# A hybrid encoder trunk on one core: the dots of the matrix memory's modulation issued with the third and fourth head's values only, each kept in its place, and two gate steps two products later

## The chip, the cores and the metric

The kernel is one program on one core of a Trainium2 chip. Its time is the device time of one execution in microseconds (us), as the median of the runs shown. A profile is one execution taken by the hardware profiler; its times are counted from the first instruction of the program. The engines are named as in the profile: PE is TensorE, PEld its weight load, DVE VectorE, ACT ScalarE, POOL GpSimd, SP SyncE, which issues the loads and stores.

## The reference

The trunk has two layers over 1024 tokens of width 1024, all in float32. The first mixes tokens by latent attention, the second by a matrix memory; each is followed by a gated MLP. Every sub-layer takes a modulation from the conditioning vector: a shift, a scale and a gate, which are six products of one vector with a 1024 x 1024 matrix per layer. Of the second layer, this is what the change touches (cut):

```python
mod = c_act @ mod_w[i] + mod_b[i]
sh_a, sc_a, g_a, sh_f, sc_f, g_f = [t[:, None, :] for t in jnp.split(mod, 6, axis=-1)]
h = rms_norm(x) * (1 + sc_a) + sh_a
...
proj = h @ w_in
q, k, v, o, gates = jnp.split(proj, [qk_w, 2 * qk_w, 2 * qk_w + v_w, 2 * qk_w + 2 * v_w], axis=-1)
i_pre, f_pre = gates[..., :H], gates[..., H:]
log_f = jax.nn.log_sigmoid(f_pre)
bc = lax.cumsum(gate_chunks(log_f), axis=3)
...
C_new = decay[..., None, None] * C + jnp.einsum('bhs,bhsv,bhsd->bhvd', ws, vt, kt)
```

The matrix memory has four heads, with 128 wide keys and 256 wide values. For each head the sequence is gone through in chunks; from chunk to chunk a state C is carried, weighted by what the gates give. While the second layer's memory is computed, the kernel also has to compute three of its modulation vectors: the gate `g_a` of this sub-layer, and the scale and shift of the MLP behind it.

## The kernel before, in words

**Products.** Everything is computed from float32 split into a high and a low part (`whi` and `wlo` for weights). Each product of 128 rows is three matmuls (`mm3`, lines 175 to 177): high by high, high by low, low by high. A weight of 128 x 1024 comes by `unit`: a 512 KB load into a raw buffer `wraw`, a copy on ScalarE to the high part (line 167), a subtraction on VectorE to the low part (line 168). In this part of the program there are two raw buffers and four pairs of split ones.

**Order.** The code is written in the order in which it should run, but a list scheduler with its own picture of durations sets the final order of each engine, and it may move an instruction ahead of others. `tc.keep_in_program_order` keeps an instruction where the code has it. Each engine, SyncE too, runs its instructions strictly in the final order.

**Modulation dots.** `mod_dot` (line 198) is one VectorE instruction over 128 x 1024 numbers: a piece of the modulation matrix, loaded into a tile `mraw`, times the activated conditioning vector (`crow`, here a copy `crow2`), summed to one number per partition. `mod_steps` yields after each; eight of them give one vector, and `mod_bias` ends it (line 203). In the matrix memory `mraw` takes a buffer of the same ring of two as `wraw`. The 24 dots of this part are drawn two at a time (`piece(mods, 2)`) behind each of the four groups of the values of the second, third and fourth head. They aren't kept in order.

**The matrix memory.** The first head's values and the gates' raw numbers are computed first, then the four gate steps run on small tiles, each put off until a number of products (`GATES`) has been issued: `gates0` makes sums and maxima along the rows (ending in the scan of line 1562), `gates1` transposes their ends (`gr`, line 1566) and makes the maxima carried from chunk to chunk, `gates2` makes weights from them and stores two of them to memory (`gd`, line 1587), `gates3` transposes the weights to columns (`gcol`). `need(gcol)` runs whatever step is still put off when the first 20 products of the next query and key (`inp`) are through. The two stored rows come back as broadcasts (`load_rows`, line 1414: into `crow` and into `ib`, which has one buffer).

Per head there are then:
- the values (`v_proj`): four groups of 16 products of 256 columns into `vp`, each split into the tile `va` (lines 608 and 609)
- the preparation (`prep`) of two halves of the sequence, placed behind the second and the third group: the scores `st`, the transposed keys `kp`, the weighted and split `pT`, `qw` and `kw`
- the chain (`chain`): eight steps, each with products into `po` and, but for the last, `pc`, a new state C on VectorE (lines 1466 and 1468), its high part on ScalarE (1471) and its low part on VectorE (1472)
- between the chain's steps, pieces of other products, here called the cover: the output gate (`ogate`, tile `inp`, two weights for a head), which needs nothing of the chain
- query and key of the next head, and `finish`, which transposes the result (`yT`).

Of the kernel before, what the change touches and what calls it, by code (L numbers as in the profile page):

```python
# [42 lines left out]
WARM = 14  # L43
W0, W0_RSTD, WF, WF_RSTD = (6, 10), (4, 3), (4, 5), (4, 6)
SHARE = 7
GATES = (2, 16, 20, 24)
MODS = (0,) * 4 + (2,) * 11 + (3,)
BS = 3
K_SSQ, K_ROWS, K_ROPE, K_NORM = 2, 4, 3, 3
# [48 lines left out]
def trunk_kernel(ctx: ExitStack, tc: tile.TileContext, xT, pos, c_d, cols_d, mod_w, win, winT, w0, w1, wf, wd, out):  # L98
# [98 lines left out]
    def mod_dot(l, i, raw, c=None):  # L197
        return dve.scalar_tensor_tensor(raw, raw, 1.0, crow if c is None else c, ALU.mult, ALU.mult, accum_out=modc[l][:, i:i + 1])
# [6 lines left out]
    def mod_steps(parts, raw_tile, c=None):  # L205

        for l, j in parts:
            for k in range(KT):
                raw = raw_tile()
                nc.sync.dma_start(raw, mod_w[l, j * 8 + k])  # L210
                if c is None:
                    yield
                    tc.keep_in_program_order(mod_dot(l, j * 8 + k, raw))
                else:
                    mod_dot(l, j * 8 + k, raw, c)
                    yield
            mod_bias(l, j * 8, KT)

# [552 lines left out]
    mods = mod_steps(((0, 2), (0, 4), (0, 3)), lambda: mod_raw())  # L771
# [32 lines left out]
    def piece(gen, n=1):  # L804
        for _ in range(n):
            next(gen, None)
# [478 lines left out]
    mods = mod_steps(((0, 5), (1, 1), (1, 0)), lambda: pF[0].tile([P, D], F32, tag="mraw", bufs=1, name=nm("mraw")))  # L1285
# [79 lines left out]
    def v_proj(hd):  # L1365
        va = va_tiles()
        uv = [unit(w1[U_MV + 2 * hd + i]) for i in range(2)]
        yield va
        for t2 in range(4):
            ps = mm_tile("vp")  # L1370
            for j in range(2):
                t = 2 * t2 + j
                tsl = slice((t % 4) * P, (t % 4 + 1) * P)
                for k in range(KT):
                    rs = [x[:, (k % 4) * 256:(k % 4 + 1) * 256] for x in uv[k // 4]]
                    mm3(ps[:, j * 256:(j + 1) * 256],
                        (h[t // 4][0][:, k, tsl], h[t // 4][1][:, k, tsl]), rs, k == 0, k == KT - 1)
            ps3 = ps.rearrange("p (a b) -> p a b", a=2)
            split_ps(va[0][:, 2 * t2:2 * t2 + 2, 0:256], va[1][:, 2 * t2:2 * t2 + 2, :], ps3)
            piece(mods, 2)  # L1380
            yield va

    def in_steps(u, hf, evac):
# [394 lines left out]
```

## Time and profile before

| | |
|---|---|
| three runs, median | 2217.82 us (2212.6 to 2218.76) |
| the profiled execution | 2215.57 us |
| its span, first to last instruction | 2213.9 us |
| mean granted TensorE clock | 0.992 |
| TensorE matmuls busy | 2169.1 us, 98% |
| VectorE busy | 1698.4 us, 77% |
| the 56 dots that load into `mraw` | median 1.219 us each |

The rows of the profile name the line, the engine, the operation, the tile written and the tiles read. Behind a bar stand a group's busy time, the mean of one in ns, and the engine's idle time just before, with what ended it. In a timeline a row begins with its start and its length, and a bracket gives the idle time before it and what ended that. In a table by windows a row begins with the window, its length, and for each engine the busy time with the number of instructions, then the granted clock, the share of the DMA engines that was busy, and GB/s.

### The profile page before, as it was taken

What the parts mean: (1) busy time and instruction counts of PE and PEld (TensorE: products, weight loads), DVE (VectorE), ACT (ScalarE), POOL (GpSimd) and SP (SyncE); (2) the same over time, 40 slices, a digit from 0 to 9 for tenths busy, and PEclk for the clock granted to TensorE, in tenths of its full rate; (3) what the DMA queues carried; (4) which work ended last, traced back from release to release, by engine and by line L of the source; (5) the groups of instructions that cost most, each with busy time, mean ns of one, the idle gap of its engine ahead of it and who ended that gap; (6) DMA issues with size and microseconds to landing.
All of it is one profiled execution on the core that took longest, in us unless ns stands there. A gap on an engine that the chain in (4) does not pass through costs nothing.

```text
span 2213.9 us, 28734 instructions
## 1 busy us (share of the span) xinstructions
PE 2169.1 (98%) x10553; PEld 1819.7 (82%) x10553; DVE 1698.4 (77%) x2754; ACT 1045.3 (47%) x1812; POOL 200.4 (9%) x232
## 2 busy tenths in 40 slices
PE   9999999999999999999999999999999999999997
PEld 7878888887888888778888888988788888877886
DVE  8877788669878776999974755466887777689996
ACT  6466566456444444443353434344554444444335
POOL 0000000000000000242210111010000000022222
PEclk9999999999999999999999999999999999999998
DMA  8412334832444442543133342354243332245122
GB/s 315 151 50 64 99 101 154 281 114 66 158 140 141 132 131 80 190 150 99 48 114 104 104 130 70 119 176 149 67 134 100 110 124 96 82 157 205 43 66 77
DMA packets 105085, 270.50 MB, mean 122 GB/s; under 512 B 12336, under 2 KB 15984, under 8 KB 104944
## 3 DMA queue, kind: packets, MB, share of 16 engines
q1 hardware_dynamic: 104544, 268.28, 37.1%
q8 instruction: 83, 1.36, 0.3%
q14 instruction: 58, 0.48, 0.1%
q10 hardware_dynamic: 400, 0.39, 0.1%
HBM read 221.53 MB, written 44.47 MB: 120 GB/s over the span
## 4 chain that ended last, share of the span: by engine, by line
PE 87%; DVE 7%; DMA 2%; ACT 1%; issue 1%; POOL 0%; SPq 0%; DVEq 0%; POOLq 0%; ACTq 0%
PE pa L177 7%; PE pa L175 7%; PE pa L176 7%; PE pd L175 4%; PE pd L176 4%; PE pd L177 4%; PE sc L677 3%; PE da L175 3%; PE da L177 3%; PE da L176 3%; PE op L175 3%; PE op L177 3%; PE op L176 3%; PE db L177 2%; PE inp L177 2%; PE inp L175 2%
## 5 line engine op out<-in xcount | busy, mean ns | idle before, releaser
L992 ACT ACTIVATE whi<-raw 128x512 fp32r<-128x512 f32 (+1 forms) x252 | 147.5, 607 | 262.4 <-PE pb L176 61.0
L992 ACT ACTIVATE whi<-wsum 128x512 fp32r<-128x512 f32 (+1 forms) x224 | 133.9, 617 | 184.1 <-PE pa L176 61.5
L175 PE MATMUL pa<-T,whi 128*128 128x512 f32 x528 | 206.6, 391 | 5.0 <-DVE g L1080 5.0
L177 PE MATMUL pa<-T,wlo 128*128 128x512 f32 x528 | 206.5, 391 | 3.1 <-DVE wlo L993 3.1
L176 PE MATMUL pa<-T,whi 128*128 128x512 f32 x528 | 205.9, 390 | 0.0
L993 DVE TENSOR_TENSOR wlo<-wsum,whi 128x512 fp32r<-128x512 f32 (+1 forms) x224 | 150.7, 686 | 33.2 <-ACT whi L992 31.8
L993 POOL TENSOR_TENSOR wlo<-raw,whi 128x512 fp32r<-128x512 f32 (+1 forms) x96 | 140.8, 1480 | 382.6 <-ACT whi L992 341.2
L175 PE MATMUL da<-U,whi 128*128 128x512 f32 (+1 forms) x364 | 139.8, 384 | 2.2 <-ACT whi L992 2.2
L176 PE MATMUL da<-U,whi 128*128 128x512 f32 (+1 forms) x364 | 139.1, 382 | 0.0
L177 PE MATMUL da<-U,wlo 128*128 128x512 f32 (+1 forms) x364 | 138.4, 382 | 0.0
L993 DVE TENSOR_TENSOR wlo<-raw,whi 128x512 fp32r<-128x512 f32 (+1 forms) x156 | 104.7, 678 | 24.9 <-ACT whi L992 24.9
L167 ACT ACTIVATE whi<-wraw 128x1024 fp32r<-128x1024 f32 x67 | 70.7, 1058 | 112.0 <-PE op L176 59.8
L175 PEld LDWEIGHTS pa<-T,whi 128*128 128x128 f32 x528 | 99.4, 188 | 28.0 <-DVE g L1080 4.1
L177 PEld LDWEIGHTS pa<-T,wlo 128*128 128x128 f32 x528 | 99.5, 188 | 24.6 <-DVE wlo L993 4.0
L176 PEld LDWEIGHTS pa<-T,whi 128*128 128x128 f32 x528 | 99.4, 188 | 20.5
L1143 DVE TENSOR_TENSOR U<-q,U 128x1024 fp32r<-128x1024 f32 x84 | 108.2, 1307 | 6.0 <-ACT U L1142 5.5
L1032 ACT ACTIVATE ct<-a,cols 128x512 f32<-128x512 f32 x88 | 71.0, 808 | 87.7 <-DVE a L1054 47.9
L168 DVE TENSOR_TENSOR wlo<-wraw,whi 128x1024 fp32r<-128x1024 f32 x67 | 82.4, 1233 | 36.2 <-ACT whi L167 34.2
L177 PE MATMUL db<-U,wlo 128*128 128x512 f32 x264 | 102.7, 390 | 1.7 <-DVE wlo L993 1.7
L175 PE MATMUL db<-U,whi 128*128 128x512 f32 x264 | 103.7, 393 | 0.0
L176 PE MATMUL db<-U,whi 128*128 128x512 f32 x264 | 102.8, 389 | 0.0
L176 PE MATMUL inp<-h,whi 128*128 128x512 f32 x256 | 100.3, 393 | 0.4 <-DVE h L282 0.4
(378 smaller groups left out, 6083.9 us busy)
## 6 DMA issues: line engine op xcount, KB each, us to landing
raw<-in_wf SPq DMA_DIRECT2D x96, 512.0 KB, 4.0
wraw<-in_w SPq DMA_DIRECT2D x67, 512.0 KB, 3.6
mraw<-in_mod_w SPq DMA_DIRECT2D x56, 512.0 KB, 3.6
ud<-ct SPq DMA_DIRECT2D x88, 256.0 KB, 2.2
q<-ud SPq DMA_DIRECT2D x88, 256.0 KB, 3.9
raw<-in_wd SPq DMA_DIRECT2D x32, 512.0 KB, 5.5
pa<-in_mod_w SPq DMA_DIRECT2D x24, 512.0 KB, 3.7
x<-xd SPq DMA_DIRECT2D x48, 256.0 KB, 4.6
```

The lines of the kernel that those rows point to most:

```text
L167: act.activation(hi, raw, AF.Copy)
L168: dve.tensor_tensor(lo, raw, hi.bitcast(F32), ALU.subtract)
L175: pe.matmul(ps, lh, rh, start=first, stop=False, skip_group_check=more)
L176: pe.matmul(ps[:, 0:rl.shape[-1]], lh, rl, start=False, stop=False, skip_group_check=more)
L177: pe.matmul(ps, ll, rh, start=False, stop=last, skip_group_check=more)
L677: pe.matmul(ps[:, cs], a[:, qs if n < 3 else qrs_], b[:, cs], start=n == 0, stop=n == 4)
L992: act.activation(hi, src, AF.Copy)
L993: eng.tensor_tensor(lo, src, hi.bitcast(F32), ALU.subtract)
L1032: act.activation(t, a[:, 2:], AF.Identity, bias=col(f"cb{l}", m), scale=cw(m, 2))
L1143: dve.tensor_tensor(lo, w, hi.bitcast(F32), ALU.subtract)
```

## The change

The dots are no longer drawn behind the second head's values; behind the third and fourth head's they come three at a time, twelve for each head, so that there are still 24. Each is kept in program order, as the dots elsewhere in the kernel were. Of the numbers in `GATES` the last three are raised by two.

```diff
-GATES = (2, 16, 20, 24)
+GATES = (2, 18, 22, 26)
...
                 if c is None:
                     yield
-                    tc.keep_in_program_order(mod_dot(l, j * 8 + k, raw))
-                else:
-                    mod_dot(l, j * 8 + k, raw, c)
+                tc.keep_in_program_order(mod_dot(l, j * 8 + k, raw, c))
+                if c is not None:
                     yield
...
-            piece(mods, 2)
+            if hd > 1:
+                piece(mods, 3)
             yield va
```

In the changed kernel lines behind 213 and ahead of 1379 have a number lower by one. Three places show what the scheduler makes of it.

VectorE at the gates, before. The tile `crow` holds the gates' rows, `mraw` is a piece of the modulation, and the scan of line 1562 appears under the name of its instruction's form:

```order
L1560 SCALAR_TENSOR_TENSOR crow<-one,crow 32x128
L1561 TENSOR_TENSOR crow<-crow 32x128
L198 SCALAR_TENSOR_TENSOR mraw_11022,modc_80<-mraw_11022,crow_10217 128x1024
L1562 SCALAR_TENSOR_TENSOR crow<-crow 32x128
L1568 COPY grow<-gr_10552 1x64
L1571 SCALAR_TENSOR_TENSOR mend<-grow 1x8 x4
L1574 COPY mprow<-mend 1x4x7
L168 TENSOR_TENSOR wlo_10968<-wraw_10965,whi_10967 128x1024
L1580 COPY mp<-gp_10582 32x1
L198 SCALAR_TENSOR_TENSOR mraw_11025,modc_80<-mraw_11025,crow_10217 128x1024
L1581 TENSOR_SCALAR crow<-crow,mp 32x128
```

The same place in the changed kernel:

```order
L1560 SCALAR_TENSOR_TENSOR crow<-one,crow 32x128
L1561 TENSOR_TENSOR crow<-crow 32x128
L1562 SCALAR_TENSOR_TENSOR crow<-crow 32x128
L168 TENSOR_TENSOR wlo_10968<-wraw_10965,whi_10967 128x1024
L1568 COPY grow<-gr_10566 1x64
L1571 SCALAR_TENSOR_TENSOR mend<-grow 1x8 x4
L1574 COPY mprow<-mend 1x4x7
L1580 COPY mp<-gp_10582 32x1
L1581 TENSOR_SCALAR crow<-crow,mp 32x128
```

The two dots are gone, and the split of a weight has moved ahead of the copy of `gr`. The other six dots that stood further down in the first head are gone too; on TensorE `gr` stands six matmuls later than before, and the first chain step 20 matmuls of `inp` earlier.

VectorE at the third head's values, before, from the low part of the first group on:

```order
L609 TENSOR_TENSOR va_11739<-vp_11753,va_11738 128x512
L609 TENSOR_TENSOR va_11739<-vp_11811,va_11738 128x512
L1433 TENSOR_TENSOR crow<-crow,st_11874 128x512
L1434 TENSOR_TENSOR qT_11594<-qT_11594,ib_11145 128x512
L612 SCALAR_TENSOR_TENSOR kw_11895<-kp_11881,gcol,kw_11894 128x128
L1404 TENSOR_TENSOR pT_11887<-crow,pT_11886 128x512
L1404 TENSOR_TENSOR qw_11891<-qT_11594,qw_11890 128x512
```

In the changed kernel:

```order
L608 TENSOR_TENSOR va_11715<-vp_11729,va_11714 128x512
L198 SCALAR_TENSOR_TENSOR mraw_11780,modc_80<-mraw_11780,crow_10217 128x1024
L198 SCALAR_TENSOR_TENSOR mraw_11783,modc_80<-mraw_11783,crow_10217 128x1024
L198 SCALAR_TENSOR_TENSOR mraw_11786,modc_80<-mraw_11786,crow_10217 128x1024
L608 TENSOR_TENSOR va_11715<-vp_11789,va_11714 128x512
L198 SCALAR_TENSOR_TENSOR mraw_11840,modc_80<-mraw_11840,crow_10217 128x1024
L1433 TENSOR_TENSOR crow<-crow,st_11855 128x512
L1434 TENSOR_TENSOR qT_11570<-qT_11570,ib_11133 128x512
L611 SCALAR_TENSOR_TENSOR kw_11876<-kp_11862,gcol,kw_11875 128x128
L1404 TENSOR_TENSOR pT_11868<-crow,pT_11867 128x512
L198 SCALAR_TENSOR_TENSOR mraw_11843,modc_80<-mraw_11843,crow_10217 128x1024
L1404 TENSOR_TENSOR qw_11872<-qT_11570,qw_11871 128x512
```

Before, the eight dots of this group stood ahead of the third head's values, among the last chain steps of the second head and its results; now twelve stand between the values and the preparation, the last two of them behind the chain's first new states. In SyncE's order the twelve loads stand in one row, with two pairs of `load_rows` among them, and the load of the output gate's first weight, which stood ahead of the values' first group, comes behind all twelve. The fourth head has the same pattern.

TensorE at the third head's chain, before, from its first step on (`po` and `pc` are the chain's products, `inp` the cover):

```order
L175 MATMUL po_12062<-va_11738,pT_11886 128x258
L176 MATMUL po_12062<-va_11739,pT_11886 128x256
L177 MATMUL po_12062<-va_11738,pT_11887 128x258
L175 MATMUL pc_12066<-va_11738,kw_11894 128x258
L176 MATMUL pc_12066<-va_11739,kw_11894 128x256
L177 MATMUL pc_12066<-va_11738,kw_11895 128x258
L175 MATMUL inp_12084<-h_9799,whi_12080 128x512
L176 MATMUL inp_12084<-h_9800,whi_12080 128x512
L177 MATMUL inp_12084<-h_9799,wlo_12081 128x512
```

In the changed kernel:

```order
L175 MATMUL po_12050<-va_11714,pT_11867 128x258
L176 MATMUL po_12050<-va_11715,pT_11867 128x256
L177 MATMUL po_12050<-va_11714,pT_11868 128x258
L175 MATMUL pc_12054<-va_11714,kw_11875 128x258
L176 MATMUL pc_12054<-va_11715,kw_11875 128x256
L177 MATMUL pc_12054<-va_11714,kw_11876 128x258
L175 MATMUL po_12085<-va_11714,pT_11867 128x258
L176 MATMUL po_12085<-va_11715,pT_11867 128x256
L177 MATMUL po_12085<-va_11714,pT_11868 128x258
L175 MATMUL pc_12092<-va_11714,kw_11875 128x258
```

Before, twelve matmuls of cover follow each chain step; now 45 products of the chain stand ahead of the first matmul of the cover. In the fourth head it is 48.

## The prediction

> **What bounds the kernel now.** The page comes first: its span, the busy times and the chain that ended last.
>
> ```profile
> span 2213.9 us, 28734 instructions
> PE 2169.1 (98%) x10553; PEld 1819.7 (82%) x10553; DVE 1698.4 (77%) x2754; ACT 1045.3 (47%) x1812; POOL 200.4 (9%) x232
> PE 87%; DVE 7%; DMA 2%; ACT 1%; issue 1%; POOL 0%; SPq 0%; DVEq 0%; POOLq 0%; ACTq 0%
> ```
>
> TensorE is the path almost everywhere, so an edit is worth what it adds to or takes from TensorE's idle time. All that is moved lies in the matrix memory, between 1200 and 1465 us. Two windows give TensorE's busy time there (span, then PE busy), up to the end of the second head's first chain step and from there on; then the view of waits, for 1150 to 1600 us, names what TensorE waited for.
>
> ```profile
> 1200.00:1274.00 74.00, 67.12 (x448) 60.05 (x449) 54.53 (x138) 34.79 (x84) 8.39 (x10) 1.00 0.40 124
> 1274.00:1465.00 191.00, 188.01 (x1139) 167.62 (x1140) 98.32 (x217) 74.56 (x168) 21.21 (x23) 1.00 0.32 96
> PE gr L1566 <- DVE crow L1562: 2.3, 1, 2.3
> PE po L177 <- DVE pT L1404: 2.3, 1, 2.3
> PE po L176 <- DVE C L1472: 2.0, 3, 0.8
> PE po L175 <- ACT C L1471: 1.9, 2, 1.5
> PE po L175 <- ACT pT L1403: 0.6, 1, 0.6
> ```
>
> In the first stretch 74.00 - 67.12 = 6.9 us are idle: that is all the change can win there. In the second, 191 us with the third and fourth heads, only 3.0 us are idle (2.1 of them at the start of the third head's chain, 1.5 + 0.6). There is little to win there and much to lose.
>
> **First head: what the removed dots give.** VectorE's timeline at the gates and, 20 us on, ahead of the first chain step:
>
> ```profile
> 1200.67 1.21 DVE L198 SCALAR_TENSOR_TENSOR mraw<-mraw,crow 128x1024 f32<-128x1024 f32 x1
> ...
> 1201.81 0.41 DVE L1562 TENSOR_TENSOR_SCAN crow<-crow 32x128 f32<-32x128 f32 x1
> ...
> 1222.79 1.64 DVE L198 SCALAR_TENSOR_TENSOR mraw<-mraw,crow 128x1024 f32<-128x1024 f32 x1
> ...
> 1224.36 0.68 DVE L1404 TENSOR_TENSOR pT<-crow,pT 128x512 fp32r<-128x512 f32 x1
> ```
>
> A dot stands ahead of the scan that the row of maxima (gr) waits for, and another ahead of the low part of pT. Without the first the scan ends at 1201.1 instead of 1202.2. The gate step moved by two products stands six matmuls later on TensorE; the row of products below gives 16.50 / 72 = 0.23 us each, so it is reached at 1202.2 - 2.3 + 1.4 = 1201.3: the wait of 2.3 us goes. The other two edited numbers can do little: the program calls the rest of the gates after 20 products at the latest, as before. The dot's removal also takes away the 2.3 us on pT.
>
> ```profile
> 1307.10:1323.60 16.50, 16.50 (x72) 13.34 (x72) 1.18 (x2) 1.00 0.57 176
> 1207.27 3.65 DMA gd<-crow
> 1211.42 6.64 DMA ib<-gd
> 1220.83 0.39 PE L175 MATMUL po<-va,pT 128*128 128x258 f32 x1 [0.57 <-ACT pT L1403]
> ```
>
> What is late next is the gates' way through memory (two pieces of the chain, and the first chain step on TensorE): 3.65 us to write the rows, up to 6.64 to read them back. It starts about 3.4 us earlier (the wait of 2.3 us is gone, and so is the second dot, which held VectorE 1.14 us, as 1200.67 to 1201.81 shows for the first, ahead of the gates' last products), and the read shares its queue with no modulation load; I take 1 to 2 us less for it. But in the new order the first chain step stands 20 matmuls earlier on TensorE (20 x 0.23 = 4.6 us), which with the 2.3 us makes it arrive at 1220.3 - 6.9 = 1213.4, while pT, ready at 1220.8 now, is ready between 1215.5 and 1217.4. I take 3 us of wait there, 1 us for the first state (its copy stands behind the product with the second row, ib, whose one buffer is refilled late), and 0.8 elsewhere: 4.8 of the 6.9 stay. **Gain 2.1 us**, between 0 (all of it turns into waits for the rows) and 6.9.
>
> **Third and fourth head: what the pinned dots cost.** Twelve dots each now stand between the values, and twelve loads of 512 KB go through the two raw buffers that the weights use too. A load is issued only when the dot two before it has read its buffer. The trace shows that pace where four dots of the old second group follow each other (VectorE, with the wait for the load in brackets), with the loads' landing times in that stretch (us from issue), and over all 56 of them:
>
> ```profile
> 1388.11 1.23 DVE L198 SCALAR_TENSOR_TENSOR mraw<-mraw,crow 128x1024 f32<-128x1024 f32 x1 [2.02 <-DMA mraw<-in_mod_w]
> ...
> 1399.35 1.22 DVE L198 SCALAR_TENSOR_TENSOR mraw<-mraw,crow 128x1024 f32<-128x1024 f32 x1 [1.34 <-DMA mraw<-in_mod_w]
> mraw<-in_mod_w SPq DMA_DIRECT2D x4, 512.0 KB, 4.3
> wraw<-in_w SPq DMA_DIRECT2D x1, 512.0 KB, 3.7
> DMA to landing us min/median/max: 3.3/3.6/7.6
> ```
>
> Four dots in 11.24 us, 2.81 us each. Now the stretch that must hide them: the third head's values on TensorE (busy time of that tile, x192), the low part of their first group on VectorE, and the split of a weight on ScalarE:
>
> ```profile
> 1323.50:1349.30 25.80, 23.63 (x192) 23.09 (x191) 2.07 (x3) 1.78 (x3) 1.00 0.22 73
> 1330.12 0.69 DVE L609 TENSOR_TENSOR va<-vp,va 128x512 fp32r<-128x512 f32 x1 [4.36 <-ACT va L608]
> L167 ACT ACTIVATE whi<-wraw 128x1024 fp32r<-128x1024 f32 x37 | 39.2, 1060 | 73.7 <-PE op L176 33.4 <-PE inp L176 24.3 <-DMA wraw<-in_w 13.5
> ```
>
> Time runs from 1330.1, where the first low part begins. The values end on TensorE at +19.2. The first two dots have their loads in the buffers already: they run from +0.6, 1.15 us apart (1.14 above). Nine more at 2.81 bring the eleventh to +0.6 + 1.15 + 25.3 = +27.0, and its end to +28.2. Only then can the raw buffer take the first weight of the output gate, which is what TensorE works on between the chain's steps: +0.1 to issue, 3.7 to land, 1.06 to split: +33.1. In the old order that weight was in before the values began. From +19.2 to +33.1 TensorE has 45 products of 256 or 258 columns (the order's rows, 23.63 / 192 = 0.12 each: 5.5 us) and nothing else: 13.9 - 5.5 = 8.4 us idle, where 2.1 are now. **Cost 6.3 us.** The fourth head has 48 such products (5.9 us) and no idle time there now: **cost 8.0 us**. The second weight waits for the twelfth dot and has 44 matmuls, 10 us, of cover; nothing is late after it. The dots taken from the stretches between heads free VectorE where it waited: worth nothing.
>
> Can VectorE itself keep that pace? Its groups from 1323 to 1404 us:
>
> ```profile
> L612 DVE SCALAR_TENSOR_TENSOR kw<-kp,gcol,kw 128x128 fp32r<-128x128 f32 x8 | 2.8, 348 | 1.7 <-ACT kw L611 1.7
> L609 DVE TENSOR_TENSOR va<-vp,va 128x512 fp32r<-128x512 f32 x4 | 2.8, 690 | 10.5 <-ACT va L608 10.5
> L1434 DVE TENSOR_TENSOR qT<-qT,ib 128x512 f32<-128x512 f32 x2 | 1.4, 685 | 0.0
> L1404 DVE TENSOR_TENSOR qw<-qT,qw 128x512 fp32r<-128x512 f32 x2 | 1.4, 685 | 0.0
> L1404 DVE TENSOR_TENSOR pT<-crow,pT 128x512 fp32r<-128x512 f32 x2 | 1.4, 682 | 0.0
> L1433 DVE TENSOR_TENSOR crow<-crow,st 128x512 f32<-128x512 f32 x2 | 1.4, 677 | 0.0
> ```
>
> Splits and preparation are 11.2 us, eleven dots 12.7: 23.9 us without a wait, which puts the eleventh dot's end at +24 even if every load were there. So the cost has a floor: cover at +24 + 0.1 + 3.3 + 1.06 = +28.5, idle 3.8 and 3.4, cost 1.7 and 3.4 us. For the ceiling, each pair is held up 1 us by the broadcast rows that stand between the loads in SyncE's queue, and VectorE's own work falls into the waits badly: 4 us later, cost 10.3 and 12.0.
>
> The idle time has a price of its own. Windows (span, PE busy; the number after POOL's, or ahead of the last two, is the granted clock):
>
> ```profile
> 9.00:12.00 3.00, 2.05 (x4) 1.36 (x5) 2.94 (x5) 1.73 (x3) 0.00 (x0) 0.60 1.05 350
> 12.00:16.00 4.00, 4.00 (x11) 3.07 (x11) 3.66 (x6) 3.62 (x8) 0.00 (x0) 0.50 1.03 394
> 1222.00:1225.00 3.00, 0.83 (x4) 0.36 (x2) 3.00 (x6) 0.39 (x2) 1.15 (x1) 1.00 0.32 72
> 1601.00:1605.00 4.00, 4.00 (x14) 3.15 (x13) 4.00 (x8) 2.67 (x4) 0.00 (x0) 0.67 0.44 131
> ```
>
> At 1601 to 1605, all work, a clock of 0.67 lost (1 - 0.67) x 4 = 1.3 us; at 9 to 16 us 0.60 and 0.50 lost 1.2 + 2.0 = 3.2; the 2.2 idle us of 1222 to 1225 lost nothing. Eight idle us in fourteen are more than any of these. I take 1.3 us a head (2.6 us at half clock once the cover starts), between 0 and 3.2. **Cost 2.6 us.** The Trainium skill ("TensorE: Matmul & The Clock Gate", Part 1) says that the clock is halved after an idle window of about 3.4 us and comes back after about 3.4 us of work; by that the sum would have 1.7 us a head in place of 1.3, and these windows agree with it.
>
> **The sum**, against the profiled execution (2215.57 us, 1.7 above its span): -2.1 + 6.3 + 8.0 + 2.6 = +14.8, that is 2230.4. The three timed runs have their median 2.25 higher, at 2217.82; I halve the difference and forecast **2231 us**.
>
> **Rivals.**
>
> 1. *The first head decides.* Place: the gates and the first head's chain. All 6.9 us of idle time there go, and the later heads hide their dots: 2215.6 - 6.9 = 2208.7. The point that decides is the pace of the dots: the cover must be in by 19.2 + 5.5 + 2.1 = +26.8, so the eleventh dot must end by +21.9, a pace of 2.1 us. For it: waits on VectorE's removed dots are there to see. Against it: 2.81 measured, and VectorE's own work ends at +24. Chance 0.05.
> 2. *Loads land at their best, 3.3 us, every time.* A pair then takes 3.3 + 1.25 = 4.55 us, 2.3 a dot, and VectorE's floor of +24 holds instead: costs 1.7 + 3.4, clock 0 to 2.6, gain 2.1: 2218.6 to 2221.2, most of it within 0.3%. Against it: two loads under way took 4.3. The Trainium skill ("DMA: Bandwidth & Descriptors", Anatomy of one DMA) gives a load 2.0 us plus its bytes at 436 GB/s, for loads that GpSimd issues: an estimate of 3.2 us for 512 KB; the median of 3.6 here is above it. Chance 0.12.
> 3. *The ceiling*: 10.3 + 12.0, clock 3.2 a head, gain 2.1: +26.6, 2242. Chance 0.15.
> 4. Forecast as worked out, with half to one and a half of its two costs: 2223 to 2238. Chance 0.65. The rest, 0.03, for what I don't see. That the dots aren't pinned, or the loads keep their place, is ruled out by the new order's rows.
>
> **How the numbers follow.** About 0.3%, 6.6 us, is what a measurement of this kernel can tell from no change: 2211 and 2224.4 are the bounds. Faster: rival 1 and 0.01 of the rest, 0.06. Within: most of rival 2 and the forecast's low end, 0.12. Slower: 0.82. The range from 2219 to 2243 takes in rivals 2 and 3 nearly to their ends and leaves out rival 1 and some of the tails.
>
> **What would show it.** Right: TensorE's wait for gr is gone; before the first cover matmul of the third and of the fourth head it waits 6 to 10 us in all, and the last of that is for ScalarE's whi, behind a load issued after the eleventh dot; the granted clock falls below 1.00 in both places; the dots come 2.6 to 3 us apart. Wrong: a cover weight that lands before the values end, dots 2 us apart, or a first head that loses more than it does now.

## The result, and the profile after

Six runs of the changed kernel have their median at 2227.18 us (2225.35 to 2231.92), six of the kernel before, on the same chip, at 2217.48 us. The ratio is 1.0052, 95% interval 1.0042 to 1.0062: slower by half a per cent (the medians lie 9.7 us apart, the ratio makes 11.5). The profiled execution of the changed kernel took 2227.73 us, where the prediction's sum gave 2230.4. Its page, the same three rows as of before:

```profile
span 2226.0 us, 28738 instructions
PE 2174.6 (98%) x10553; PEld 1823.3 (82%) x10553; DVE 1696.9 (76%) x2754; ACT 1044.2 (47%) x1812; POOL 198.9 (9%) x232
PE 83%; DVE 9%; DMA 4%; ACT 2%; issue 2%; POOL 0%; SPq 0%; DVEq 0%; POOLq 0%; ACTq 0%
```

The number of matmuls and of VectorE's instructions is the same; TensorE is busy 5.5 us longer, since some of its products ran slower, as shown below. In the chain that ended last four per cent of the span have gone from TensorE, most of them to VectorE and the DMAs. Where the time was lost, is read from five matmuls that both kernels have: the first of the first head's values (`vp`), the first chain product (`po`) of the second, third and fourth head, and the first of the output projection (`op`). TensorE's timeline of before, then of the changed kernel:

```profile
1165.36 0.28 PE L175 MATMUL vp<-whi,h 128*128 128x264 f32 x1
...
1269.17 0.28 PE L175 MATMUL po<-va,pT 128*128 128x258 f32 x1
...
1349.16 0.28 PE L175 MATMUL po<-va,pT 128*128 128x258 f32 x1
...
1431.03 0.28 PE L175 MATMUL po<-va,pT 128*128 128x258 f32 x1
...
1464.44 0.48 PE L175 MATMUL op<-oh,whi 128*128 128x512 f32 x1
```

```profile
1164.49 0.28 PE L175 MATMUL vp<-whi,h 128*128 128x264 f32 x1
...
1263.15 0.28 PE L175 MATMUL po<-va,pT 128*128 128x258 f32 x1
...
1343.23 0.28 PE L175 MATMUL po<-va,pT 128*128 128x258 f32 x1
...
1433.34 0.28 PE L175 MATMUL po<-va,pT 128*128 128x258 f32 x1
...
1478.00 0.49 PE L175 MATMUL op<-oh,whi 128*128 128x512 f32 x1
```

Four stretches lie between them. A, with the gates and the first head's chain, went from 103.8 to 98.7 us: 5.1 won. B, with the second head's chain, is 80.0 and 80.1. C, the third head's chain and what follows up to the fourth head's, went from 81.9 to 90.1: 8.2 lost. D, the fourth head's chain, from 33.4 to 44.7: 11.2 lost. Together +14.4; the memory began 0.9 us earlier in this execution, and behind it 1.5 us were saved, so the span is 12.1 longer. Those 1.5 are about what the window of half clock cost that before had at 1600 us, one of the rows of the prediction, and that this execution of the changed kernel has not; it isn't an effect that I can lay to the change.

What TensorE waits for in the memory (view of waits, 1150 to 1600 us):

```profile
PE pc L175 <- ACT po L1474: 6.0, 2, 3.1
PE po L175 <- DVE kw L611: 2.8, 2, 2.1
PE po L176 <- DVE C L1472: 2.3, 4, 0.8
PE pc L175 <- DVE C L1466: 1.2, 1, 1.2
```

The waits for gr and for pT's low part are gone. In their place stand waits for the results of the chain itself: with nothing between its steps, TensorE waits for each.

The third head from the first low part on, from the timelines of VectorE, SyncE, ScalarE and TensorE: the first dot, the eleventh, the load of the output gate's first weight behind it (merged with the loads that follow, x4), ScalarE's copy of a chain product ahead of the split, the split, and the first matmul of the cover. The last four rows are the fourth head's load, copy, split and cover, whose first low part began at 1414.30.

```profile
1324.19 0.69 DVE L608 TENSOR_TENSOR va<-vp,va 128x512 fp32r<-128x512 f32 x1 [21.40 <-ACT va L607]
1324.80 1.22 DVE L198 SCALAR_TENSOR_TENSOR mraw<-mraw,crow 128x1024 f32<-128x1024 f32 x1
...
1351.91 1.22 DVE L198 SCALAR_TENSOR_TENSOR mraw<-mraw,crow 128x1024 f32<-128x1024 f32 x1 [0.69 <-DMA mraw<-in_mod_w]
...
1353.17 10.61 SPq L164 DMA_DIRECT2D wraw<-in_w  x4
...
1357.97 0.39 ACT L1473 ACTIVATE ob<-po 128x258 f32<-128x258 f32 x1 [1.70 <-PE po L177]
...
1358.25 1.05 ACT L167 ACTIVATE whi<-wraw 128x1024 fp32r<-128x1024 f32 x1
...
1359.35 0.74 PE L175 MATMUL inp<-h,whi 128*128 128x512 f32 x1
...
1443.94 8.09 SPq L164 DMA_DIRECT2D wraw<-in_w  x3
...
1448.52 0.39 ACT L1473 ACTIVATE ob<-po 128x258 f32<-128x258 f32 x1 [1.48 <-PE po L177]
...
1449.12 1.05 ACT L167 ACTIVATE whi<-wraw 128x1024 fp32r<-128x1024 f32 x1
...
1450.22 0.50 PE L175 MATMUL inp<-h,whi 128*128 128x512 f32 x1
```

The forecast's order of events holds: the eleventh dot ends at 1353.1 and the weight's load is issued at 1353.17. The cover starts 35.2 us behind the first low part (1359.35 - 1324.19), where 33.1 were forecast; in the fourth head 35.9 us.

### The profile page after: what moved, and what is told of

Read it like the earlier page. It is cut to its first block, busy times and chain, and to the rows that moved or that the text cites. A ratio compares the mean times of both kernels' runs of the same rounds, so it can differ in the third digit from the quotient of the medians.

```text
span 2226.0 us, 28738 instructions
## 1 busy us (share of the span) xinstructions
PE 2174.6 (98%) x10553; PEld 1823.3 (82%) x10553; DVE 1696.9 (76%) x2754; ACT 1044.2 (47%) x1812; POOL 198.9 (9%) x232
## 4 chain that ended last, share of the span: by engine, by line
PE 83%; DVE 9%; DMA 4%; ACT 2%; issue 2%; POOL 0%; SPq 0%; DVEq 0%; POOLq 0%; ACTq 0%
PE pa L177 7%; PE pa L175 7%; PE pa L176 7%; PE pd L175 4%; PE pd L176 4%; PE pd L177 4%; PE da L175 3%; PE da L177 3%; PE da L176 3%; PE sc L676 3%; PE op L175 2%; PE op L176 2%; PE op L177 2%; PE inp L175 2%; PE inp L177 2%; PE inp L176 2%
## 5 line engine op out<-in xcount | busy, mean ns | idle before, releaser
L175 PEld LDWEIGHTS pa<-T,whi 128*128 128x128 f32 x528 | 99.2, 188 | 27.9 <-DVE g L1079 4.1
L176 PEld LDWEIGHTS pa<-T,whi 128*128 128x128 f32 x528 | 99.2, 188 | 20.4
L168 DVE TENSOR_TENSOR wlo<-wraw,whi 128x1024 fp32r<-128x1024 f32 x67 | 81.9, 1224 | 35.9 <-ACT whi L167 33.8
L175 PE MATMUL db<-U,whi 128*128 128x512 f32 x264 | 103.8, 393 | 0.0
```

The costliest lines, as they stand in the source:

```text
L168: dve.tensor_tensor(lo, raw, hi.bitcast(F32), ALU.subtract)
L175: pe.matmul(ps, lh, rh, start=first, stop=False, skip_group_check=more)
L176: pe.matmul(ps[:, 0:rl.shape[-1]], lh, rl, start=False, stop=False, skip_group_check=more)
```

## The experiments

Twelve kernels, all on the same chips as runs of the kernel before. The times are medians, the ratios are against before with their 95% intervals; stretches A to D come from each one's profiled execution by the same five matmuls. One execution need not lie at its median: e5's is 2.9 us below it, the fastest of seven, e9's 3.7 below, e8's 4.2 above. The kernels with narrow dots or narrow loads leave out seven eighths of each dot's sum.

| kernel | us | ratio | A | B | C | D | C + D less before |
|---|---|---|---|---|---|---|---|
| before | | 1 | 103.8 | 80.0 | 81.9 | 33.4 | 0 |
| the change | 2227.18 | 1.0042 to 1.0062 | 98.7 | 80.1 | 90.1 | 44.7 | 19.5 |
| e1: gate numbers only | 2215.08 | 0.9987 to 1.0005 | 104.4 | 80.2 | 81.7 | 33.7 | 0.1 |
| e2: old gate numbers | 2230.75 | 1.0056 to 1.0081 | 100.4 | 80.5 | 89.7 | 44.7 | 19.1 |
| e3: not pinned | 2211.70 | 0.9971 to 0.9989 | 99.2 | 80.0 | 81.7 | 33.5 | -0.1 |
| e4: buffers of their own | 2216.46 | 0.9995 to 1.0012 | 99.0 | 80.2 | 84.2 | 37.5 | 6.4 |
| e5: narrow dots | 2221.63 | 1.0018 to 1.0040 | 98.9 | 80.2 | 86.3 | 38.1 | 9.1 |
| e6: before, pinned | 2220.84 | 1.0014 to 1.0035 | 98.7 | 84.9 | 84.3 | 38.0 | 7.1 (B: 4.9) |
| e7: narrow loads | 2224.29 | 1.0023 to 1.0050 | 98.8 | 80.0 | 87.3 | 41.9 | 14.0 |
| e8: before, narrow dots | 2213.41 | 0.9981 to 0.9999 | 101.5 | 80.5 | 83.7 | 33.7 | 2.0 |
| e9: before, narrow loads | 2212.86 | 0.9977 to 0.9996 | 99.9 | 80.4 | 81.5 | 33.5 | -0.4 |
| e10: not pinned, old gate numbers | 2211.12 | 0.9969 to 0.9987 | 100.1 | 80.3 | 81.5 | 33.4 | -0.3 |
| e11: own buffers, narrow dots | 2216.95 | 0.9996 to 1.0015 | 98.9 | 79.8 | 86.2 | 35.8 | 6.8 |
| e12: own buffers, narrow loads | 2208.29 | 0.9957 to 0.9982 | 98.7 | 80.2 | 80.4 | 34.2 | -0.7 |

The theory after the result: the cost is that the pinned dots keep the two raw buffers while the values run; the gain is that the first head has no dots. The main rival for the cost was VectorE's time for twelve dots a head, for the gain the gate numbers.

**e1**, the gate numbers alone, on the kernel before:

```diff
-GATES = (2, 16, 20, 24)
+GATES = (2, 18, 22, 26)
```

> The kernel before, with the three gate numbers raised by two and nothing else; the dots stay where they were, unpinned. Theory (the gain in the first heads, 5.15 us between the two traces, is the removal of the dots there; the gate numbers do next to nothing): TensorE reaches gr six matmuls later, 1.4 us, so about 0.9 of the 2.3 us of wait for the scan stay, the 2.3 us on pT stay, and the time is that of before within 2 us: 2216 to 2219 us. Rival (the gate numbers make the gain): both waits go and the second head's first chain step comes 5 us earlier: about 2212.5 us.

Measured: 0.9996, no difference, and A is not shorter but 0.6 longer. The profile shows why a wait removed early can be worth nothing. TensorE's timeline at gr and at the first chain step, and two windows of 3.41 us there (window, span, PE busy, and behind POOL the granted clock):

```profile
1199.76 0.18 PE L1566 MATMUL gr<-ident,crow 32*1 32x32 f32 x1 [0.63 <-DVE crow L1562]
...
1222.66 0.42 PE L177 MATMUL po<-va,pT 128*128 128x258 f32 x1 [2.27 <-DVE pT L1404]
```

```profile
1219.46:1222.87 3.41, 1.14 (x6) 0.64 (x5) 3.41 (x6) 0.49 (x2) 1.15 (x1) 1.00 0.30 104
1222.88:1226.29 3.41, 3.41 (x13) 3.04 (x13) 3.24 (x8) 2.21 (x6) 0.00 (x0) 0.50 0.83 297
```

Of the 2.3 us of wait for gr 0.6 are left, so 1.7 are won there; the 2.27 on pT's low part stay, other waits grow (1.28 in place of 0.57 on pT's high part, 0.64 new ahead of `gcol`), and a window of half clock follows that before has not. The rival falls: the gate numbers do not make the gain.

**e2**, the same question from the other side, the changed kernel with `GATES = (2, 16, 20, 24)`:

> The changed kernel, with the old gate numbers; dots as in the change. Theory: gr now stands directly behind the products it had before, and the scan is earlier by one dot, so about 1.1 us of wait for gr come back and nothing else: 2227 to 2229 us. Rival (the gate numbers make the gain in the first heads): the 5 us there are lost: about 2232 us.

Measured: A is 1.7 us longer than in the change, 1.2 of it the wait for gr that came back. The median, 2230.75, lies above the theory's 2227 to 2229 and below the rival's 2232; it is 3.6 us above the change's, but taken beside other runs of before, and the intervals against before overlap (1.0056 to 1.0081, 1.0042 to 1.0062). Inside the change the gate numbers are worth up to 1.7 us, not 5.

**e3**, the pins alone taken back; twelve dots each in the third and fourth head as in the change:

```diff
-                tc.keep_in_program_order(mod_dot(l, j * 8 + k, raw, c))
-                if c is not None:
+                    tc.keep_in_program_order(mod_dot(l, j * 8 + k, raw))
+                else:
+                    mod_dot(l, j * 8 + k, raw, c)
                     yield
```

> The changed kernel, but the dots of this part aren't kept in program order: the scheduler may move them, as before; still twelve each for the third and fourth head, three to a group. Theory (the cost is that the pinned dots keep the two raw buffers while the values run, so that the output gate's first weight comes late and the chain runs bare): the weight's load comes back ahead of the values, TensorE idles less than 3 us in each of the two heads, the granted clock stays at 1.00 there, and the 5 us of the first heads stay won: about 2212 us, between 2210 and 2216. Rival (VectorE's time for twelve dots a head, wherever they stand): 8 and 11 us of cost stay in good part: 2220 to 2227 us.

Measured: 2211.70 us, 0.2% faster than before (0.9971 to 0.9989) and as forecast. All the cost is gone and 4.6 of the 5.1 us in A stay. The scheduler puts nearly all dots ahead of the values, and SyncE issues the output gate's weights behind them, three at 1323.57 to 1330.27 with the values still running. The view of waits of TensorE, 1300 to 1480 us, has the chain waits of before again:

```profile
PE po L175 <- ACT C L1472: 1.4, 1, 1.4
PE po L176 <- DVE C L1473: 0.6, 1, 0.6
```

So neither three dots to a group nor twelve to a head cost anything as long as the scheduler may move them: the pin does. What of the pin, the next runs ask.

**e4**, the pins kept, the dots' loads in two buffers of their own:

```diff
-                     lambda: wp.tile([P, 1024], F32, tag="wraw", bufs=wraws, name=nm("mraw")), crow2)
+                     lambda: pm.tile([P, 1024], F32, tag="mraw", bufs=2, name=nm("mraw")), crow2)
```

> The changed kernel, but the dots' loads have two raw buffers of their own and no longer share the weights' two; the dots stay pinned where the change has them. Theory (the shared buffers make the cost): the output gate's first weight is loaded ahead of or beside the dots, its products stand between the chain's steps again, and of the 8.2 and 11.3 us that the third and fourth head cost at most 3 each stay: 2212 to 2218 us. Rival (VectorE's time: twelve pinned dots of 1.15 us among splits, preparation and first states): the chain's first steps are still late for VectorE and 2222 to 2227 us stay.

Measured: 2216.46, as fast as before. C and D lose 6.4 us instead of 19.5; the cover stands behind the chain's first step again (1343.64 and 1427.82), and the granted clock is 1.00 throughout. Two thirds of the cost, 13.1 us, are the shared buffers. The third head keeps 2.3, inside the 3 us expected, the fourth 4.0, a little more.

**e5 and e7** divide the pace of the dots. In e5 the loads are whole and each dot runs over 128 columns; in e7 each load is 64 KB and each dot runs over 1024 numbers (the 128 loaded columns repeated, the products into a tile of their own).

```diff
-        return dve.scalar_tensor_tensor(raw, raw, 1.0, crow if c is None else c, ALU.mult, ALU.mult, accum_out=modc[l][:, i:i + 1])
+        n = D if c is None else P
+        return dve.scalar_tensor_tensor(raw[:, 0:n], raw[:, 0:n], 1.0, (crow if c is None else c)[:, 0:n], ALU.mult, ALU.mult, accum_out=modc[l][:, i:i + 1])
```

```diff
-                nc.sync.dma_start(raw, mod_w[l, j * 8 + k])
+                nc.sync.dma_start(raw if c is None else raw[:, 0:P], mod_w[l, j * 8 + k] if c is None else mod_w[l, j * 8 + k][:, 0:P])
```

> The changed kernel, with the dots of this part over the first 128 of the 1024 columns only (seven eighths of each dot's sum are left out); the loads stay whole and go through the same two raw buffers. A dot then takes VectorE some 0.2 us in place of 1.22. Theory (loads through two shared buffers hold the output gate's weight back): the dots follow at the pace of the loads alone, about 4 us a pair plus issue, 2.1 to 2.3 us a dot, the eleventh ends 20 to 24 us behind the first low part, and a good half of the cost in the third and fourth head stays: 2219 to 2225 us, and the clock still falls below 1.00 in the bare chain. Rival (VectorE's time is the cost): the two heads take what they took before: 2211 to 2214 us.

> The changed kernel, with the loads of this part's dots cut to the first 128 of the 1024 columns, 64 KB in place of 512; each dot still multiplies and sums 1024 numbers on VectorE (those 128, eight times over; seven eighths of the matrix piece are left out). The loads still go through the same two raw buffers, ahead of the output gate's first weight. Theory: with the wait for 512 KB gone the dots follow at VectorE's own work, the eleventh ends about 24 us behind the first low part in place of 28.9, and the cost falls to 2 to 4 us in the third and 3 to 6 us in the fourth head, with less clock lost: 2216 to 2222 us. Rival (VectorE's time alone is the cost): nothing changes, 2224 to 2228 us. Rival (the transfer alone is the cost): both heads as before, 2211 to 2213 us.

Measured: e5 2221.63, inside its 2219 to 2225; e7 2224.29, 2 us above its 2216 to 2222 and just inside the first rival's 2224 to 2228. By its time alone e7 can't be told from the change (1.0023 to 1.0050 and 1.0042 to 1.0062); the stretches tell them apart. Of the 19.5 us, 9.1 stay with dots that take next to no time, and 14.0 with loads that are an eighth: neither VectorE's time nor the loads alone make the cost. The third head of e7, VectorE's timeline of the first low part and the eleventh dot:

```profile
1325.09 0.69 DVE L611 TENSOR_TENSOR va<-vp,va 128x512 fp32r<-128x512 f32 x1 [21.40 <-ACT va L610]
...
1348.21 1.22 DVE L200 SCALAR_TENSOR_TENSOR mjunk<-mraw,crow 128x1024 f32<-128x1024 f32 x1
```

The eleventh dot ends 24.3 us behind the first low part, which is the floor of +24 that the prediction worked out from VectorE's groups. In e5 the eleventh dot comes at 1352.21 with the first low part at 1325.75, +26.5, later than the expected 20 to 24: two buffers, loads that landed 4.1 us after issue (median, 3.3 to 6.4), and rows between them. e7 lost 5.5 us in the third head and 8.5 in the fourth, 1.5 and 2.5 beyond the expectation, and most of that is clock. The first stretch of the cover in the third and in the fourth head:

```profile
1354.94:1357.61 2.67, 2.67 (x10) 2.28 (x10) 2.65 (x6) 2.67 (x7) 0.09 (x1) 0.50 0.28 63
...
1442.20:1446.37 4.17, 4.17 (x13) 3.40 (x13) 2.71 (x4) 1.90 (x5) 0.00 (x0) 0.50 0.36 132
```

The cover began at 1354.94 and 1442.20, and its first 2.67 and 4.17 us ran at half clock: 1.3 and 2.1 us.

**e6**, the kernel before with the pins and nothing else (its old gate numbers too); eight dots behind the values of each of the second, third and fourth head:

```diff
                 if c is None:
                     yield
-                    tc.keep_in_program_order(mod_dot(l, j * 8 + k, raw))
-                else:
-                    mod_dot(l, j * 8 + k, raw, c)
+                tc.keep_in_program_order(mod_dot(l, j * 8 + k, raw, c))
+                if c is not None:
                     yield
```

> The kernel before, with the dots kept in program order and nothing else: two for each group of the second, third and fourth head, eight a head, none in the first; the old gate numbers. Theory: the first head gains what the old gate numbers leave of it, about 3.5 us; in each of the three other heads the seventh dot ends some 17 to 19 us behind the first low part, the output gate's weight is split at 21 to 24, where the values end at 19, so the chain has 30 bare products and 1 to 3 us more idle time a head: 2215 to 2222 us. Rival (what costs is three dots to a group, or the twelve of a head, on VectorE): no head loses, 2212 to 2214 us. Rival (any pinned head costs as the third and fourth do in the change): 2217 - 3.5 + 3 x 8 = 2237 us.

Measured: 2220.84, within 2215 to 2222. A fell by 5.1 us with the old gate numbers, more than the 3.5 expected: without dots the first head has its gain either way. Each of the three pinned heads pays, 4.9, 2.5 and 4.6 us, two of them above the 1 to 3 expected, all far below 8. The cost is larger with more dots ahead of the weight, and in the kernels with shared buffers it can be counted in one way: the time from a head's first chain product to its first cover matmul, less 0.12 us for each chain product between them, less the 2.1 us that the third head waits there anyway.

| kernel and head | chain to cover, us | products | worked out | measured |
|---|---|---|---|---|
| the change, third | 1343.23 to 1359.35 | 45 | 8.6 | 8.2 |
| the change, fourth | 1433.34 to 1450.22 | 48 | 11.1 | 11.2 |
| e5, third | 1344.79 to 1358.93 | 57 | 5.2 | 4.4 |
| e5, fourth | 1431.07 to 1441.59 | 47 | 4.9 | 4.7 |
| e6, second | 1261.01 to 1269.54 | 30 | 4.9 | 4.9 |
| e6, third | 1345.91 to 1354.56 | 30 | 3.0 | 2.5 |
| e6, fourth | 1430.24 to 1439.39 | 39 | 4.5 | 4.6 |
| e7, third | 1344.13 to 1354.94 | 32 | 4.9 + 1.3 clock | 5.5 |
| e7, fourth | 1431.47 to 1442.20 | 32 | 6.9 + 2.1 clock | 8.5 |

The sum says where the time goes, not what held the cover up. In e7 that wasn't the weight: its split ended at 1354.49 and 1441.75, 0.45 us ahead of the cover, and the 32 chain products that the order puts ahead of it were not through.

**e8 and e9** ask what made the gain in A: the same two edits as in e5 and e7, on the kernel before, whose first head has eight of the dots.

> The kernel before, with the dots of this part over the first 128 of 1024 columns only (seven eighths of each sum are left out); loads whole, order free as before. It is for the first head: from the first matmul of its values to the second head's first chain product TensorE took 103.8 us before and 98.7 in the change. Theory (of those 5.1 us the larger part comes from the loads that no longer share the queue with the gates' rows, the smaller from VectorE): the two rows still take 5 to 6 us to come back, and this stretch falls by 1 to 2.5 us only, to 101.3 to 102.8; the whole 2213 to 2216 us. Rival (VectorE's time for the dots makes the gain): 98.7 to 99.7 us, the whole 2211 to 2213.

> The kernel before, with the loads of this part's dots cut from 512 to 64 KB (128 of 1024 columns); each dot still takes VectorE its 1.2 us (those columns eight times over; seven eighths of the matrix piece are left out). Again for the first head's stretch, 103.8 us before and 98.7 in the change. Theory (the loads in the queue make the larger part): the rows are written in some 2 us and read in some 4, as in the change, and the stretch falls by 2.5 to 4 us, to 99.8 to 101.3, with most of the wait for gr left; the whole 2211 to 2214 us. Rival (VectorE's time makes it): 103 to 104 us, the whole as before.

Measured: A is 101.5 in e8 and 99.9 in e9, both inside the theory's ranges (the 2.0 us of e8 in C are for the most part a window of half clock); of the 5.1 us the narrow dots give 2.3 and the narrow loads 3.9. The way of the gates' rows through memory, as the DMA issues of before, then of the change show it (the stores, then the first loads back; KB each, median us to landing):

```profile
gd<-crow SPq DMA_DIRECT2D x2, 16.0 KB, 3.4
crow<-gd SPq DMA_DIRECT2D x2, 256.0 KB, 5.9
ib<-gd SPq DMA_DIRECT2D x1, 256.0 KB, 6.6
```

```profile
gd<-crow SPq DMA_DIRECT2D x2, 16.0 KB, 1.6
crow<-gd SPq DMA_DIRECT2D x2, 256.0 KB, 4.5
ib<-gd SPq DMA_DIRECT2D x1, 256.0 KB, 4.7
```

In e8 the three are 2.0, 5.5 and 6.4 us, in e9 1.5, 4.8 and 5.0. So the rows come back in 5.5 to 6.6 us with the dots' whole loads beside them, in 4.5 to 5.0 without or with small ones. The store of 16 KB is slow where a load of 512 KB was issued just ahead of it: of the two stores the first took 3.65 us in before, 0.4 us behind such a load, 2.3 in e8, 1.6 us behind one, and 1.9 in the change, 1.8 us behind a weight's.

But the two kernels changed more than that. In before two dots stand ahead of the low part of pT (the second from 1222.79 to 1224.36), and TensorE waits 2.3 us there; in e8 and e9 the scheduler put none there, that wait is gone, and the first chain step stands 18 matmuls earlier, nearly as in the change (20). What is left of TensorE's waits in A shows the difference: in e8 1.3 us for gr and 1.7 for pT's high part, which comes after the rows, in e9 2.1 for gr and 0.3 for pT. So the wait for gr can stay nearly whole with 3.9 of the 5.1 us won; how much of these is the rows' faster way and how much the dots' new places, these runs don't separate.

**e10**, e3 with the old gate numbers:

> The unpinned kernel (twelve dots each for the third and fourth head, not kept in order), with the old gate numbers. It asks what the gate numbers are worth without the pins, and whether they belong into the best version. Theory (they are worth what they were in the pinned kernel, 1.7 us in the first head's stretch, 1.2 of it a wait for gr): 2213 to 2214 us beside 2211.7. Rival (worth nothing, since with old numbers and eight pinned dots a head the same stretch was 98.7 us too): 2211 to 2212.

Measured: A is 0.9 us longer than in e3, with 1.2 us of wait for gr; the median is 0.6 us lower, and the intervals (0.9969 to 0.9987, 0.9971 to 0.9989) are as good as the same. The time lies in the rival's 2211 to 2212; what the gate numbers are worth here can't be told. Both kernels beat before and the change; e3 and e10 are the best that compute everything, some 4.5 to 5 us below before.

**e11 and e12** ask what the 6.4 us are that stay in e4. e11 is e4 with the narrow dots of e5, e12 is e4 with the narrow loads of e7 (into buffers of 128 columns).

> Both of the supposed causes taken away together: the changed kernel with two raw buffers of the dots' own and with the dots over 128 of 1024 columns only (seven eighths of each sum are left out), dots pinned where the change has them. With buffers of their own the third and fourth head still took 6.4 us more than before (2.4 and 4.0). Theory (those 6.4 are VectorE's time for full dots that stand ahead of the chain's first states): they fall to 0 to 2 us, so the whole is 2210.5 to 2213 us. Rival (they come from the traffic or the new order and not from VectorE's time): they stay, 2215 to 2217 us.

Measured: 6.8 us stay, the whole is 2216.95. The theory of this run, that they are VectorE's time, falls. Its profile shows VectorE idle where it should have been late:

```profile
1348.09 0.48 DVE L1425 TENSOR_SCALAR crow<-crow,gcol 128x128 f32<-128x128 f32 x2 [2.69 <-DMA crow<-gd]
...
1350.48 0.28 DVE L199 SCALAR_TENSOR_TENSOR mraw<-mraw,crow 128x128 f32<-128x128 f32 x1
...
1350.69 0.42 DVE L1467 COPY C<-pc 128x258 f32<-128x258 f32 x1
```

```profile
1351.61 0.58 PE L175 MATMUL po<-C,qw 128*128 128x258 f32 x1 [4.14 <-ACT C L1472]
```

The broadcast row is late, the tenth dot stands behind it, the first new state C behind that, and TensorE waits 4.14 us for it. The granted clock then fell to a half from 1350.1 to 1356.9, with TensorE at work through the last 5.3 us of it: that is some 2.6 of the 6.8 us. Without them 4.2 would stay, still above the theory's 0 to 2.

> The counterpart to the run with own buffers and narrow dots, in which 6.8 us stayed in the third and fourth head: own raw buffers for the dots, loads cut to 64 KB (128 of 1024 columns), the dots full for VectorE (those columns eight times over; seven eighths of the matrix piece are left out), pinned as in the change. Theory formed after that run (what stays beside the shared buffers is the traffic: twelve loads of 512 KB a head in SyncE's queue hold up the broadcast rows, and the pinned dots stand ahead of first states while they wait for theirs): with small loads at most 3 of the 6.4 to 6.8 us stay in the two heads, the whole 2210 to 2213.5 us. Rival (VectorE's full dots ahead of the first states cost the same by themselves): 5 to 7 us stay, 2215 to 2217 us.

Measured: 2208.29, below the expected 2210 to 2213.5, and nothing of the 6.4 us is left (-0.7); TensorE's longest wait in the third and fourth head's chains is 0.4 us. So full dots pinned among the values cost nothing by themselves. Two thirds of the cost are loads that hold the weights' buffers (13.1 us), the rest loads of 512 KB that keep VectorE waiting (6.4 us). For what it waits, differs: in e11's third head for a broadcast row behind them in SyncE's queue, in e4's for the load of a dot that stands ahead of the state's low part, VectorE's and then TensorE's timeline:

```profile
1353.77 1.23 DVE L198 SCALAR_TENSOR_TENSOR mraw<-mraw,crow 128x1024 f32<-128x1024 f32 x1 [1.32 <-DMA mraw<-in_mod_w]
...
1354.92 0.42 DVE L1472 TENSOR_TENSOR C<-C,C 128x258 fp32r<-128x258 f32 x1
```

```profile
1355.40 0.39 PE L176 MATMUL po<-C,qw 128*128 128x258 f32 x1 [1.09 <-DVE C L1472]
```

e12 takes both away, so it doesn't say which of them weighs more.

## Why the prediction was right, and where its terms were off

The direction and the mechanism were right: pinned dots hold the raw buffers, the cover's weight comes late, the chain runs bare, and that costs more than the first head wins. That the total fits so closely is luck, since two of its terms are off in opposite directions.

**The late weight** (forecast 6.3 + 8.0, measured, clock included, 8.2 + 11.2). The steps up to the weight's landing held: the eleventh dot was forecast to end at +28.2 and ended at +28.9 and +29.5, the cover's weight was issued behind it, and its load took 3.8 and 3.5 us where 3.7 were forecast (the view of tile `wraw` from 1353 to 1354 and from 1443.5 to 1444.2 us):

```profile
DMA to landing us min/median/max: 3.8/3.8/3.8
```

```profile
DMA to landing us min/median/max: 3.5/3.5/3.5
```

Mis-sized was the step from landing to split, which the prediction put at nothing. The weight was there at 1357.0 and 1447.4, and its split began at 1358.25 and 1449.12, 1.2 and 1.7 us later: ScalarE's order has copies of the chain's results ahead of it, and the copies of 1357.97 and 1448.52 waited for a product of TensorE. With 0.7 for the dots, 0.1 for the load and 1.2 for this, +33.1 becomes +35.1, of 35.2 measured. In the fourth head the dots end 0.6 later again. The prediction's figure from the Trainium skill ("DMA: Bandwidth & Descriptors", Anatomy of one DMA), an estimate of 3.2 us for these bytes, is below both loads; the measurement decides.

Nor did TensorE wait for the weight alone. The chain products that its order puts ahead of the cover, 45 and 48, ended at 1359.22 and 1450.25, when the weight's splits ended too (1359.30 and 1450.17). So in this order the weight itself held TensorE for 0.13 us in the third head and not at all in the fourth. The shared buffers act through the order as well: with buffers apart, in e4, the cover stands behind the chain's first step. No run has the change's order with an early weight; e7 comes nearest, where the weight was early, only 32 products stood ahead, and 14.0 of the 19.5 us stayed.

The dots' ten steps, forecast at 2.64 us on average ((1.15 + 25.3) / 10), measured 2.71 in the third head ((1351.91 - 1324.80) / 10). That VectorE's own work puts the eleventh dot near +24 fits e7, +24.3, with 0.7 us of wait for a load in it. There were two bounds close to each other, loads and VectorE: that is why e5 and e7 gave back only 10.4 and 5.5 of the 19.5 us, and rival 2, which took one of them away by faster loads, would have been too cheap: with 64 KB loads the cost was still 14.0.

**The first head** (forecast 2.1, between 0 and 6.9; measured 5.1). The step that failed is "pT ... is ready between 1215.5 and 1217.4. I take 3 us of wait there". The first chain product ran at 1212.9 with half a us of wait. I had allowed 1 to 2 us for the way of the rows through memory without the loads beside it. It was 3.7: 1.8 for the store (3.4 to 1.6) and 1.9 for the read of ib (6.6 to 4.7). The wait of 2.3 us on pT's low part went with the dots ahead of it, as forecast. e8 and e9, 2.3 won with VectorE's dots cut and 3.9 with the loads cut, add up to more than 5.1, so each saves part of the same time; with the dots in other places too they don't give the parts.

**The clock** (forecast 2.6, at half clock once the cover starts; on the traces between 0.3 and 3.2 us). The granted clock did halve in both heads, for 10.2 us each, but earlier than I placed it, over the bare chain. TensorE's windows from 1346 to 1363 us in the change:

```profile
1346.24:1349.65 3.41, 1.25 (x6) 0.83 (x6) 3.15 (x8) 1.62 (x6) 0.00 (x0) 1.00 0.89 295
1349.65:1353.07 3.42, 2.08 (x8) 1.79 (x8) 2.73 (x8) 0.84 (x2) 0.00 (x0) 0.50 0.79 233
1353.07:1356.48 3.41, 2.72 (x11) 2.43 (x12) 3.10 (x10) 1.85 (x7) 0.00 (x0) 0.50 0.59 193
1356.48:1359.89 3.41, 3.28 (x14) 2.95 (x14) 2.38 (x10) 1.92 (x5) 0.00 (x0) 0.50 0.53 155
1359.89:1363.30 3.41, 3.41 (x18) 2.84 (x17) 3.41 (x8) 1.89 (x4) 1.77 (x2) 1.00 0.48 132
```

The chain's products took 0.21 us each instead of 0.12 there. The cover starts at 1359.35, and full clock is back at 1359.89, so only 0.54 us of cover ran at half clock, a loss of 0.3; in the fourth head none. But ScalarE's copies ahead of the split waited for products that ran at half clock, so some of the 1.2 and 1.7 us between landing and split may be the clock's as well, at most 2.9 in the two heads. No run has the bare chain at full clock, so this stays open. The forecast's 2.6 lies inside, but not where it was placed. The price of half clock is that of the work that it slows on the path: in e7, where the cover started earlier, it was 1.3 and 2.1 us on the cover.

**The sum.** Forecast -2.1 + 14.3 + 2.6 = +14.8; measured -5.1 + 0.1 + 8.2 + 11.2 = +14.4, with the clock in the last two. The total was good to 0.4 us in the memory because the first head's gain was 3 us too small and the late weight, taken together with the clock, 2.6 too cheap. Rival 1, that the first head decides, had its gain nearly right (5.1 of 6.9) and failed where it was said to, at the pace of the dots. Of the signs named, the dots' pace, the clock and gr came as forecast; TensorE's waits before the cover are 6.1 and 6.3 us (the other 4 to 5 us of each went into slow products), and the last of them is for ScalarE's split in the third head only, 0.13 us; in the fourth the chain and the split end together. That sign came only in part: the waits are mostly for the chain's own results.

## What to carry to other kernels

An instruction that is kept in its place keeps its load's buffer too: ask which load takes that buffer next, and price the pin by the moment when that load can be issued. A load that has landed isn't used yet: look for what stands ahead of its reader on the reader's engine. Where a chain has cover, its cost is the time from the chain's start to the cover's start, less the chain's own products; here that sum holds within a microsecond in nine heads of four kernels. And before the end of a wait is credited, look at the other ways to the same point: with the wait for gr shortened by 1.7 us nothing was won in e1, and with 2.1 us of it still there 3.9 us were won in e9.

## What the runs showed of the hardware

The granted clock fell after windows that were far from idle. In the change the window ahead of the fall, 1346.24 to 1349.65, has 1.25 of 3.41 us busy, and no single wait of TensorE's was longer than 3.1 us; in e1 it was 1.14 busy of 3.41, in e5 (1433.24 to 1436.65) 2.29. In before a window with 1.50 busy did not make it fall:

```profile
1221.33:1224.75 3.42, 1.50 (x9) 0.96 (x7) 3.42 (x7) 0.89 (x2) 1.15 (x1) 1.00 0.27 56
```

So these rows give no share of busy time that decides. The Trainium skill ("TensorE: Matmul & The Clock Gate", Part 1) speaks of an idle window of about 3.4 us ahead of the half clock; the window's length agrees with these rows, its idleness doesn't. The prediction read from the same page that the clock comes back after as much work; in the change it came back only behind windows that were nearly full, 3.28 and 3.2 of 3.41, and stayed at a half behind 2.08 and 2.72, so that a chain with gaps kept it for three windows in each head.

The other: two 16 KB stores took 3.4 us (median) to land in before, the first 0.4 us behind a 512 KB load in the same queue, and 1.6 in the change, the first 1.8 us behind one.
